# A two-layer decoder trunk on one core: every tile's row in SBUF rounded up to 128 bytes

## Chip, core and metric

The kernel runs on one core of one Trainium2 chip. Its time is what the device takes for one execution, in microseconds (us); the median of the runs counts. Five engines work side by side, each through its own list of instructions: TensorE (matmuls, PE in the rows; the load of a matmul's weights is PEld), VectorE (DVE), ScalarE (ACT), GpSimd (POOL) and SyncE (SP, which here only issues DMAs).

## What is computed

The reference is a decoder trunk with two layers on x of 256 x 1024 in float32. In each layer:

```python
h = rms_norm(x, norm_mix_pre[l])
proj = h @ w_in[l]                       # 1024 x 11776
q, k, v, lru_x, lru_gate, glu_in, gate_logits = jnp.split(proj, IN_SPLITS, axis=-1)
y_a = dilated_attention_mixer(q, k, v, cos, sin, w_o_attn[l])
y_b = rg_lru_mixer(lru_x, lru_gate, ..., w_o_lru[l])
y_c = conformer_conv_mixer(glu_in, conv_dw_w[l], ..., w_o_conv[l])
g = jax.nn.sigmoid(gate_logits).reshape(B, S, N_BRANCHES, D)
merged = g[:, :, 0] * y_a + g[:, :, 1] * y_b + g[:, :, 2] * y_c
x = x + rms_norm(merged @ w_out[l], norm_mix_post[l])
h = rms_norm(x, norm_mlp_pre[l])
u = jnp.square(jax.nn.relu(h @ w_mlp_up[l]))
x = x + rms_norm(u @ w_mlp_down[l], norm_mlp_post[l])
```

Nearly all the arithmetic is in products with weights; about 100 MB of them are read for each layer.

## The kernel before

**Chunks.** The weights come as one stream of 92 chunks a layer, each 128 partitions x 2,048 floats (1 MB). SP loads a chunk into a `raw` buffer (two of them, L428). ScalarE rounds it to the type fp32r, which gives `whi` (L392), and VectorE makes `wlo = raw - whi` (L405); of each there are three buffers. The activations are split in the same way (`hh` and `hl` for h, `uh` and `ul` for the squared ReLU, and so on). Each product is then three fast fp32r matmuls, whi x hi, whi x lo and wlo x hi, summed in PSUM (L452).

**Two shapes of matmul.** In chunks of the kind "ws" (lx, lg, glu, q, k, ga, gb, gc, oa, ob, oc, up: 64 of a layer) the weights are the stationary operand and 256 columns of the activations move past them: 48 matmuls a chunk. In those of the kind "as" (v, wo, ua, dn: 28 of a layer) the activations are stationary and 512 columns of weights move: 24 matmuls a chunk. Every matmul loads 128 columns of its stationary operand. The gate products of the recurrent branch (psr, psi) and the last-but-two chunk of the MLP of layer 0 (dn61, which is kept for later) have their split weights not in `whi` and `wlo` but in general slots. Attention (sc, tp, pv) and the sums of the layer norm are plain fp32 matmuls on smaller tiles; transposes (L459) move `ident` past the data.

**Buffers.** A `Buf` is one logical tile with a tag; all tiles with one tag share that tag's buffers, whose number is `cap[tag]`. The tile is taken from its pool when it is first used, in `View.ap`. The pools lay their buffers one behind another along the row of a partition. `cp` holds constants (x_sb, nhalf with 8 bytes, halfpi with 4, const with 4,100 and others), `wp` raw, whi and wlo, `sp` the rest: gains, xp (2,080 bytes), upad, 24 slots with tag s2 of 2,048 bytes, statistics (tag st, 4 bytes), hh and hl, cpd, sm and pT. `pp` is PSUM.

**Order.** A planner in `Sched.run` simulates the engines with a cost for each operation and writes out one fixed order for each engine, from shapes, costs and the number of buffers; the main matmuls follow a list (`ORDER`). Background work of VectorE and ScalarE, the taps of the convolution with 31 taps, fills the gaps.

Of the kernel before, what the change touches and what calls it, by code (L numbers as in the profile page):

```python
# [100 lines left out]
DMA_RATE = 0.36  # L101
MARGIN = 15000
DMA_ISSUE, DMA_START, DMA_DONE = {"SP": 600, "POOL": 1040, "ACT": 600}, 500, 900
RINGS = ("mm", "tp", "sc", "raw", "whi", "wlo", "upad", "xp", "sm", "pT")


class Buf:
    def __init__(self, sch, pool, shape, dt, tag, name):
        self.sch, self.pool, self.shape, self.dt, self.tag, self.name = sch, pool, shape, dt, tag, name
        self.t = None  # L110
        self.log = []
        self.left = 0
        self.held = False
        self.uses = []

    def __getitem__(self, idx):
        if not isinstance(idx, tuple):
            idx = (idx,)
        reg, n = [], 1
        for i, d in enumerate(self.shape):  # L120
            e = idx[i] if i < len(idx) else slice(None)
            if isinstance(e, int):
                reg.append((e, e + 1))
            else:
                r = range(*e.indices(d))
                reg.append((r[0], r[-1] + 1))
                if i:
                    n *= len(r)
        return View(self, tuple(reg), n, lambda t: t[idx])
# [21 lines left out]
class View:  # L151
# [10 lines left out]
    def ap(self):  # L162
        b = self.buf
        if b.t is None:
            b.t = b.pool.tile(list(b.shape), b.dt, tag=b.tag, name=b.name, bufs=b.sch.cap[b.tag])
        return self.fn(b.t)

    @property
    def psum(self):
        return self.buf.tag in ("mm", "tp", "sc")  # L170


class Op:
# [8 lines left out]
class Sched:  # L182
# [45 lines left out]
    def run(self):  # L228
# [4 lines left out]

        for tag in RINGS:
            ring, c = self.rings[tag], self.cap[tag]
# [1074 lines left out]
```

## Time and profile before

| | us |
|---|---|
| runs | 1141.12 median of 3 (1139.95 to 1143.14) |
| profiled execution, span from its first to its last instruction | 1141.4 |
| TensorE busy in it | 1118.9 |
| VectorE busy | 904.4 |
| ScalarE busy | 720.9 |

The profile shows one execution. What lies around its span is within the spread of the runs: the span and their median differ by 0.3 us. Matmuls overlap, so that a matmul's own duration (about 280 ns for 256 columns) says little; how far the starts of two of them lie apart is what sums to the time.

### The profile page before, as it was taken

Reading aid. Unit: us, or ns where it says so; the run is one execution under the profiler, and the core shown is the slowest. Engines: PE = TensorE matmul, PEld = TensorE weight load, DVE = VectorE, ACT = ScalarE, POOL = GpSimd, SP = SyncE. Lnnn points to the kernel's source line nnn. Section 1 sums busy time; section 2 is a strip of 40 time slices with the busy share of each in tenths; the row PEclk is TensorE's granted clock in tenths of the full one; section 3 lists DMA queues with packets and bytes.
Section 4 is the critical chain, followed back from the end, with each engine's and each line's share of the span. In section 5 each row is a group of like instructions: output and inputs, shape, how many; then the busy total and the mean of one; then the engine's idle time right before and its main releaser. Section 6 shows DMA issues by size and latency. Waiting matters only on the chain.

```text
span 1141.4 us, 20586 instructions
## 1 busy us (share of the span) xinstructions
PE 1118.9 (98%) x8258; PEld 1038.8 (91%) x8258; DVE 904.4 (79%) x1374; ACT 720.9 (63%) x1173; POOL 76.3 (7%) x168
## 2 busy tenths in 40 slices
PE   7999999999999999999999999999999999999995
PEld 6999999999999899989889999999998988889984
DVE  6999999999869865555579999999995888555552
ACT  5779938687765464444468896569776646444441
POOL 1000022111000010000010000221200001000000
PEclk9999999999999999999999999999999999999998
DMA  8654376554345565554455443755624365545541
GB/s 291 237 203 149 146 244 208 185 180 146 129 180 190 186 220 185 184 185 185 184 200 207 168 184 128 252 201 194 214 90 174 136 240 185 187 183 188 193 173 37
DMA packets 37649, 209.76 MB, mean 184 GB/s; under 512 B 6449, under 2 KB 9777, under 8 KB 14130
## 3 DMA queue, kind: packets, MB, share of 16 engines
q1 hardware_dynamic: 32976, 200.05, 49.0%
q0 software_dynamic: 4576, 8.40, 2.2%
q8 instruction: 65, 1.06, 0.4%
q14 instruction: 30, 0.25, 0.1%
q10 hardware_dynamic: 2, 0.00, 0.0%
HBM read 201.08 MB, written 1.05 MB: 177 GB/s over the span
## 4 chain that ended last, share of the span: by engine, by line
PE 83%; DVE 8%; DMA 4%; ACT 3%; issue 1%; SPq 1%; POOL 0%; DVEq 0%; POOLq 0%; ACTq 0%
PE dn L452 16%; PE up L452 14%; PE glu L452 8%; PE v L452 6%; PE gc L452 4%; PE ga L452 4%; PE oc L452 4%; PE lx L452 4%; PE wo L452 4%; PE lg L452 4%; PE k L452 3%; PE oa L452 2%; PE ua L452 2%; PE ob L452 2%; PE pv L452 1%; PE tp L459 1%
## 5 line engine op out<-in xcount | busy, mean ns | idle before, releaser
L405 DVE TENSOR_TENSOR wlo_dn<-raw_dn,whi_dn 128x1024 fp32r<-128x1024 f32 (+1 forms) x66 | 75.8, 1189 | 70.2 <-ACT whi_dn L392 70.2
L392 ACT CAST whi_dn<-raw_dn 128x1024 fp32r<-128x1024 f32 (+1 forms) x66 | 64.4, 1022 | 77.2 <-PE dn L452 45.1
L409 DVE SCALAR_TENSOR_TENSOR c<-upad,parh,c 128x256 f32<-128x256 f32 x256 | 110.3, 477 | 0.1
L452 PE MATMUL up<-hh_mlp,whi_up 128*128 128x256 f32 x448 | 107.7, 280 | 0.0
L452 PE MATMUL up<-hl_mlp,whi_up 128*128 128x256 f32 x448 | 107.6, 279 | 0.0
L452 PE MATMUL dn<-whi_dn,uh 128*128 128x512 f32 x256 | 101.0, 395 | 0.0
L452 PE MATMUL dn<-wlo_dn,uh 128*128 128x512 f32 x256 | 100.8, 394 | 0.0
L405 DVE TENSOR_TENSOR wlo_up<-raw_up,whi_up 128x1024 fp32r<-128x1024 f32 x56 | 66.4, 1221 | 41.6 <-ACT whi_up L392 41.6
L399 ACT ACTIVATE cpd<-upad,parh 128x256 f32<-128x256 f32 x224 | 94.5, 500 | 3.3 <-DVE c L405 3.3
L452 PEld LDWEIGHTS up<-hh_mlp,whi_up 128*128 128x128 f32 x448 | 84.1, 188 | 0.7
L452 PEld LDWEIGHTS up<-hl_mlp,whi_up 128*128 128x128 f32 x448 | 84.0, 188 | 0.6
L392 ACT CAST whi_up<-raw_up 128x1024 fp32r<-128x1024 f32 x56 | 56.2, 1049 | 39.0 <-PE dn L452 21.0
L452 PE MATMUL dn<-whi_dn,ul 128*128 128x512 f32 x256 | 71.6, 394 | 0.0
L405 DVE TENSOR_TENSOR cpd<-cpd 128x1024 f32<-128x1024 f32 (+2 forms) x84 | 63.3, 773 | 0.9 <-ACT cpd L399 0.9
L452 PE MATMUL glu<-hl_mix,whi_glu 128*128 128x256 f32 x256 | 61.7, 279 | 0.0
L452 PE MATMUL glu<-hh_mix,whi_glu 128*128 128x256 f32 x256 | 61.7, 279 | 0.0
L452 PE MATMUL up<-hh_mlp,wlo_up 128*128 128x256 f32 x448 | 61.6, 279 | 0.0
L452 PEld LDWEIGHTS dn<-whi_dn,ul 128*128 128x128 f32 x256 | 47.9, 187 | 11.8
L452 PEld LDWEIGHTS dn<-whi_dn,uh 128*128 128x128 f32 x256 | 47.9, 187 | 11.1
L452 PEld LDWEIGHTS dn<-wlo_dn,uh 128*128 128x128 f32 x256 | 47.9, 187 | 11.0
L452 PEld LDWEIGHTS up<-hh_mlp,wlo_up 128*128 128x128 f32 x448 | 56.5, 188 | 0.0
L452 PEld LDWEIGHTS glu<-hh_mix,whi_glu 128*128 128x128 f32 x256 | 48.0, 188 | 0.0
(306 smaller groups left out, 3399.4 us busy)
## 6 DMA issues: line engine op xcount, KB each, us to landing
raw_dn<-w_in_stream SPq DMA_DIRECT2D x32, 1024.0 KB, 4.8
raw_up<-w_in_stream SPq DMA_DIRECT2D x28, 1024.0 KB, 4.8
raw_glu<-w_in_stream SPq DMA_DIRECT2D x16, 1024.0 KB, 4.8
raw_q<-w_in_stream SPq DMA_DIRECT2D x12, 1024.0 KB, 4.9
raw_k<-w_in_stream SPq DMA_DIRECT2D x12, 1024.0 KB, 4.8
raw_v<-w_in_stream SPq DMA_DIRECT2D x11, 1024.0 KB, 4.8
raw_lx<-w_in_stream SPq DMA_DIRECT2D x8, 1024.0 KB, 4.8
raw_lg<-w_in_stream SPq DMA_DIRECT2D x8, 1024.0 KB, 4.8
```

The costliest lines, as they stand in the source:

```text
L392: nc.scalar.copy(out.ap(), in_.ap())
L399: nc.scalar.activation(out.ap(), in_.ap(), func, scale=val(scale), **kw)
L405: lambda: nc.vector.tensor_tensor(out=out.ap(), in0=a.ap(), in1=b.ap(), op=op), [a, b], [out])
L409: lambda: nc.vector.scalar_tensor_tensor(out=out.ap(), in0=a.ap(), scalar=val(s), in1=b.ap(), op0=op0, op1=op1), [a, b] + views(s), [out])
L452: nc.tensor.matmul(out.ap(), lhsT=lhs.ap(), rhs=rhs.ap(), start=start, stop=stop)
L459: nc.tensor.transpose(out.ap(), a.ap(), ident.all().ap())
```

## The change

Each tile's row in SBUF is made longer until it is a multiple of 128 bytes; the kernel uses the part of the old length through a slice. Tiles in PSUM and the statistics (tag st: 32 buffers) are left as they are. No instruction, shape of an operand or order changes. All tiles of matmuls then begin at a multiple of 128 bytes.

```diff
+LINE = 128
+PSUM_TAGS = ("mm", "tp", "sc")
+UNPADDED = PSUM_TAGS + ("st",)
@@ class Buf
+    def home(self):
+
+        shape, row = list(self.shape), 4
+        for d in shape[1:-1]:
+            row *= d
+        last = shape[-1]
+        while self.tag not in UNPADDED and row * shape[-1] % LINE:
+            shape[-1] += 1
+        t = self.pool.tile(shape, self.dt, tag=self.tag, name=self.name, bufs=self.sch.cap[self.tag])
+        return t if shape[-1] == last else t[(slice(None),) * (len(shape) - 1) + (slice(0, last),)]
@@ class View
     def ap(self):
         b = self.buf
         if b.t is None:
-            b.t = b.pool.tile(list(b.shape), b.dt, tag=b.tag, name=b.name, bufs=b.sch.cap[b.tag])
+            b.t = b.home()
         return self.fn(b.t)
 
     @property
     def psum(self):
-        return self.buf.tag in ("mm", "tp", "sc")
+        return self.buf.tag in PSUM_TAGS
```

## Rows read from the trace of the kernel before

**Rows 1.** The page and the granted clock: span, clock, busy times, chain by engine.
```profile
core 0: 1141.4 us, clock 0.996
...
PE 1118.9 (98%) x8258; PEld 1038.8 (91%) x8258; DVE 904.4 (79%) x1374; ACT 720.9 (63%) x1173; POOL 76.3 (7%) x168
...
PE 83%; DVE 8%; DMA 4%; ACT 3%; issue 1%; SPq 1%; POOL 0%; DVEq 0%; POOLq 0%; ACTq 0%
```
**Rows 2.** The chain in order of time: start us, us, engine, tile, matmuls.
```profile
30.46 28.27 PE glu L452 x240
...
96.95 10.88 PE lg L452 x96
...
243.74 11.31 PE k L452 x96
...
260.70 11.04 PE v L452 x48
...
448.37 11.30 PE up L452 x96
459.68 11.20 PE dn L452 x48
...
802.52 10.88 PE k L452 x96
...
964.21 8.17 PE up L452 x72
```
**Rows 3.** Windows: stretch, its length, busy us by engine, granted clock, DMA.
```profile
20.00:119.00 99.00, 99.00 (x829) 98.09 (x828) 93.45 (x172) 80.58 (x138) 1.53 (x6) 1.00 0.57 207
...
203.00:282.00 79.00, 79.00 (x581) 73.82 (x581) 75.80 (x136) 60.11 (x112) 12.11 (x26) 0.98 0.51 176
...
345.00:425.00 80.00, 80.00 (x500) 71.13 (x499) 67.05 (x91) 42.95 (x64) 6.44 (x10) 1.00 0.55 199
425.00:570.00 145.00, 145.00 (x909) 129.80 (x908) 79.23 (x84) 67.23 (x85) 1.48 (x4) 1.00 0.52 188
...
768.00:845.00 77.00, 77.00 (x590) 71.55 (x589) 76.23 (x138) 60.57 (x116) 11.55 (x24) 1.00 0.54 183
...
982.00:1128.00 146.00, 146.00 (x912) 130.49 (x911) 75.31 (x79) 63.72 (x78) 0.74 (x2) 1.00 0.47 167
```
**Rows 4.** Waits: who waited for whom, us in total, times, longest.
```profile
ACT whi_dn L392 <- PE dn L452: 45.1, 13, 3.6
...
PE sc L452 <- DMA qk<-r1k: 1.8, 1, 1.8
```
**Rows 5.** VectorE's groups with 1,024 and 512 elements, shapes apart.
```profile
L405 DVE TENSOR_TENSOR wlo_dn<-raw_dn,whi_dn 128x1024 fp32r<-128x1024 f32 x62 | 73.4, 1222 | 70.2 <-ACT whi_dn L392 70.2
...
L405 DVE TENSOR_TENSOR ur<-ur 128x512 f32<-128x512 f32 x32 | 21.9, 686 | 1.5 <-ACT ur L399 1.5
```
**Rows 6.** DMA issues: tile, KB each, median us to landing.
```profile
raw_dn<-w_in_stream SPq DMA_DIRECT2D x32, 1024.0 KB, 4.8
```
**Rows 7.** Timeline of TensorE, gate products: first and last of 12 starts.
```profile
95.35 0.28 PE L452 MATMUL psr<-luh,lwh 128*128 128x256 f32 x1
...
96.67 0.28 PE L452 MATMUL psi<-luh,lwl 128*128 128x256 f32 x1
```
**Rows 8.** Timeline of TensorE, dn61: first start and that six later.
```profile
556.52 0.39 PE L452 MATMUL dn<-whi_dn,uh 128*128 128x512 f32 x1
...
557.88 0.39 PE L452 MATMUL dn<-whi_dn,uh 128*128 128x512 f32 x1
```
**Rows 9.** Timeline and group of the attention's transposes.
```profile
222.36 0.60 PE L459 MATMUL tp<-ident,sm 128*128 128x128 f32 x4
...
L459 PE MATMUL tp<-ident,sm 128*128 128x128 f32 x128 | 18.8, 274 | 1.3 <-ACT sm L399 1.3
```
**Rows 10.** The chain in order of time: pieces on VectorE and DMA.
```profile
196.58 6.03 DMA qk<-r1k
...
694.79 4.68 DVE thi L858 x8
```

## Prediction

> **What bounds the kernel now.** I read the clock and span first, then the page's busy shares and chain: TensorE is busy 98% of 1141.4 us at a granted clock of 0.996, and 83% of the chain is its matmuls [rows 1]. At 1.00 the clock is the 2.4 GHz level, so only start-up is lost to it. Second, the chain in order of time [rows 2], for the pace of the matmuls: a piece divided by its count is the spacing of two starts. This is the view that matters, since "busy" hides the pace. A chunk of 1 MB of weights is 48 matmuls of 256 columns or 24 of 512 (one layer: 64 and 28 chunks). At 2.4 GHz, 256 columns are 106.7 ns and 512 are 213.3 ns. Measured: 117.8 ns (glu 28.27/240, up 11.30/96, k 11.31/96), 113.3 ns (lg 10.88/96; k again, 10.88/96, in layer 1), 233.3 ns (dn 11.20/48), 230.0 ns (v 11.04/48) [rows 2]. So TensorE runs 4 to 10% above its column time while it waits for nobody, and k shows two paces for the same instructions on the same buffers. Over the timeline 90 of the 128 chunks with 256 columns keep the slow pace and 38 the fast one, of which the first and the last stand in [rows 2]. Third, the windows [rows 3]: VectorE is 94 to 99% busy from 20 to 119, from 203 to 282 and from 768 to 845 us, and 52 to 55% in the MLP stretches, so only the latter has plenty of room. Fourth, the waits [rows 4]: in the MLP stretch ScalarE waits for TensorE to free buffers (45.1 us before whi_dn), so preparation is ahead there.
>
> **What the change does.** It adds, removes and reorders no instruction, and the planner reads unchanged shapes. What moves is where tiles begin. Before, tiles are laid one behind another in steps of 32 bytes, and the odd rows (nhalf 8 bytes, halfpi 4, const 4,100, xp 2,080) push all later ones off: raw, whi and wlo begin 32 bytes past a multiple of 128, hh, hl, the s2 slots, sm and pT 96 past, ident 64 past. After it each begins at a multiple of 128. The padding is never read, and one row of SBUF grows by about 1.3 KB, which fits.
>
> **Cost on VectorE, ScalarE and DMA: none.** VectorE's step from 512 to 1,024 elements is 1222 - 686 = 536 ns, 1.047 ns an element [rows 5], its 0.96 GHz pace (1.042) within 0.5%; with all operands off the 128-byte grid there is nothing left per element to win. A fixed part may hide one access; bounded by that 0.5% it is 4.5 us of busy time over its 904 us, and I take 0. A chunk lands in 4.8 us [rows 6], below any chunk time here, and two raw buffers overlap; nothing to win either.
>
> **Cost on TensorE.** No row has both operands of a fast matmul on the grid, so I bound it.
> Does the address matter at all? Two places say so. The gate products psr and psi take both operands from s2 slots (both 96 past): 12 starts from 95.35 to 96.79 us (the last listed start, 96.67, plus one more), 120.0 ns each, a pace no other matmul holds for long [rows 7]. And one chunk of layer 0, dn61, keeps its split weights in s2 slots: six starts from 556.52 to 557.88 us, 226.7 ns each, where the same product from whi and wlo takes 233.3 [rows 2, 8]. Same shapes, same engine, other addresses, another pace.
> The excess also has a unit: 113.3 is 17/16 of 106.7, 120.0 is 18/16, 226.7 is 17/16 of 213.3, and 16 columns of fp32 are 64 bytes. Operands that begin 32 bytes off a 64-byte grid, as nearly all do, touch one such block more than they fill. That is my reading: the extra time is extra blocks, of the moving operand or in conflict with the weight load, and it goes when both begin on the grid.
> Price on the grid: at best the column time, 106.7 and 213.3 ns; at worst, if the address helps, the best paces seen, 113.3 and 226.7. The nearest row is the transposes: the moving operand (ident) begins on a 64-byte multiple, 128 weights are loaded each time, and four take 0.60 us with 274 ns for the last, (600 - 274)/3 = 109 ns apart [rows 9]. They are of another kind, but show load and matmul at 2.3 ns above 106.7. I take 106.7 + 2.3 = 109.0 and 213.3 + 2.3 = 215.6 ns.
> The Trainium skill (TensorE: Matmul & The Clock Gate, "Wait — 56ns, not 53.3ns?") gives columns / 2.4 GHz plus about 2.5 ns for back-to-back matmuls. By it the prices would be 109.2 and 215.8, an estimate; no run of before shows it for a fast fp32 matmul, whose rows lie above.
> Sum over both layers, per chunk: 256 columns 48 x 109.0 = 5.23 us against 5.65 (slow) or 5.44 (fast); 512 columns 24 x 215.6 = 5.17 against 5.60 (dn, wo, ua) or 5.52 (v, 8 of its 12 chunks; v0's four are like dn). So 90 x 0.42 = 37.8, 38 x 0.21 = 8.0, 48 x 0.43 = 20.6, 8 x 0.35 = 2.8, and 96 gate products x 11 ns = 1.1: together 70 us.
>
> **What takes part of it back.** A faster TensorE meets the other engines. From 119 to 203 us and from 685 to 768 us the chain runs through VectorE and the q/k copies (thi 4.68 us, a copy of 6.03 us) before a score product can start [rows 10], and TensorE already waits at its end (1.8 us [rows 4]). What it wins there it waits: about 10 fast and 4 slow chunks, 3.8 us, in layer 0, and 8 and 6, 4.2 us, in layer 1. From 203 to 282 and 768 to 845 us VectorE has 3.2 and 0.8 us of idle time [rows 3] and TensorE could win 5.0 (8 slow, 1 fast, 4 of v) and 3.5 (2, 6 and 4): 1.8 and 2.7 lost. From 20 to 119 us VectorE has 93.45 us of work and TensorE would need 99 - 7 = 92: 2 us lost. Together 14.5, say 15 us. What is late next there is VectorE's split of weights (wlo), and behind it the raw buffers and SP's loads. In the MLP (79.23 of 145 us) and the output projections (67.05 of 80) it covers. Net 70 - 15 = 55: 1141.4 - 55 = 1086. The span and the median of the runs (1141.1) differ by 0.3 us, so the time is 1086 too.
>
> **Rivals.**
> *Only the pace flips.* The extra 1/16 is in the fast fp32 matmul itself and the change only ends the conflicts: everything at 113.3 and 226.7. For it: both best paces are exactly 17/16 of the column time. Against: the transposes' 2.3 ns. 90 x 0.21 + 48 x 0.16 + 8 x 0.08 + 0.6 = 28, less 4 taken back: 1117.
> *VectorE absorbs the mixing stage.* Its queue is a fixed order, and every delay there reaches TensorE: only what follows 345 us and 902 us counts, 42 chunks a layer x 0.42 = 35: 1106. For it: 94 to 99% busy. Against: part of that work (the taps) is filler.
> *Nothing happens.* k changes its pace at unchanged addresses [rows 2], so the paces may come from the phase between load and matmul alone: 1141. The Trainium skill (SBUF — State Buffer, "Specifications (TRN2)") speaks for it: it gives lines of 16 bytes, with a penalty for each cross to a new one. Every tile already begins at a multiple of 32, so by that rule nothing changes; the 120.0 against 113.3 and the 226.7 against 233.3 don't agree with it.
> *Slower: equal remainders collide.* psr and psi are the matmuls of 256 columns whose operands have the same remainder, and they are the slowest steady ones, 120.0 [rows 7]. Afterwards all have the same one, 0. Then 90 x 48 x 2.2 ns = 9.6 and 38 x 48 x 6.7 ns = 12.2 are lost, and 48 x 0.16 = 7.7 won at 226.7: +14, 1155. It decides as soon as the 256-column spacing passes about 118. Against: dn61 has equal remainders too, and is faster for it.
>
> **How the numbers follow.** Full gain 0.47 (its own range 1070 to 1101: the lower end is 106.7 and 213.3 for all, 87 us less some 16; the upper is twice the loss), VectorE absorbs 0.09, only the flip 0.17, nothing 0.16, collision 0.11. A measurement of this kernel tells about 0.3%, 3.4 us. Faster 0.47 + 0.09 + 0.17 = 0.73; same 0.16; slower 0.11. The range reaches from 1070 to 1143 and leaves out the collision and some of the edges.
>
> **What would show it.** In the chain, dn should fall from 11.20 to about 10.4 us for 48, up from 11.31 to 10.5 for 96, glu from 28.27 to 26.2 for 240, psr to 109 ns, with no two paces left. VectorE's 1222 ns stays. TensorE's waits should grow before the score products. Wrong: the spacings unchanged (nothing), 113.3 everywhere (flip), 120 (collision), or 109 with a span above 1101 (absorbed).

## The result and the profile after

The changed kernel takes 1151.51 us (median of 4 runs, 1151.07 to 1152.12) against 1140.53 (4 runs, 1139.76 to 1143.14): a ratio of 1.0092, interval 1.0077 to 1.0106. It is slower by 0.9% or 11.0 us and lies above the predicted range, 1070 to 1143. The last rival, that operands with equal remainders collide (1155), comes within 3.5 us.

The page and the granted clock of the changed kernel, the lines that answer to [rows 1]:
```profile
core 0: 1149.6 us, clock 0.996
...
PE 1130.3 (98%) x8258; PEld 1057.6 (92%) x8258; DVE 905.1 (79%) x1374; ACT 721.8 (63%) x1173; POOL 76.2 (7%) x168
...
PE 93%; DVE 2%; ACT 2%; DMA 1%; issue 0%; POOL 0%; SPq 0%; DVEq 0%; POOLq 0%; ACTq 0%
```
The instructions are the same, and so is the mean granted clock. TensorE is busy 11.4 us longer, VectorE and ScalarE less than 1 us longer, and TensorE's share of the chain rises from 83 to 93%: it now sets the pace in stretches where others did.

The chain in order of time, for the pieces of [rows 2] (start, us, engine, tile, matmuls; the line of a matmul is now L466):
```profile
30.49 28.80 PE glu L466 x240
...
98.17 11.52 PE lg L466 x96
...
245.33 11.50 PE k L466 x96
...
451.20 11.51 PE up L466 x96
462.71 10.91 PE dn L466 x48
...
798.75 11.18 PE v L466 x48
809.93 11.50 PE k L466 x96
```
Divide each by its count: glu, lg, k and up all stand at 119.8 to 120.0 ns, where [rows 2] have 117.8 and 113.3. dn falls from 233.3 to 227.3, and k no longer has two paces. v is an exception in part: its chunks v1 and v2 take every second column of the activations as the stationary operand (a stride of 2), and they rise from 230.0 to 232.9 (11.04/48 and 11.18/48). v0 takes adjacent columns and falls with the others; in the timelines the middle spacing of its matmuls in layer 1 goes from 233 to 235 down to 227, where nothing holds it up. The gate products keep their 120.0 ns (in the timeline after, 12 starts from 96.56 to 97.88 us, 1.32 us for 11 steps).

So the two odd pairs of before, [rows 7] and [rows 8], gave the paces of the whole changed kernel but for v1 and v2, to within 0.6 ns.

What the predicted sum called free is free: VectorE's split takes 1223 ns (1222 in [rows 5]), and a chunk still lands in 4.8 us, the row of [rows 6] unchanged. The group after:
```profile
L419 DVE TENSOR_TENSOR wlo_dn<-raw_dn,whi_dn 128x1024 fp32r<-128x1024 f32 x62 | 73.4, 1223 | 69.4 <-ACT whi_dn L406 69.4
```

**Where the time went.** I added up, from the timelines of TensorE of both kernels, each matmul's start to the next start, by tile. A spacing that is over about 0.1 us too long counts as a gap; where exactly that bound lies moves up to 3 us between the rows of one kernel, and some 0.6 us between the differences.

| us, both layers | before | after | difference |
|---|---|---|---|
| 256 columns: glu, lg, lx, q, k, ga, gb, gc, oa, ob, oc, up | 723.2 | 743.9 | +20.6 |
| 512 columns from whi and wlo: dn, wo, ua | 246.4 | 240.4 | -6.0 |
| 512 columns: v | 67.5 | 67.7 | +0.2 |
| score products sc, with the waits inside them | 20.3 | 17.7 | -2.6 |
| gaps behind other main matmuls | 9.3 | 5.1 | -4.2 |

With 0.2 us of small ones this is +8.2, the difference of the two spans (1149.6 and 1141.4). The row of v holds a gain of v0 and a loss of v1 and v2. The medians differ by 11.0. In every run that lists both, the time is 1.7 to 1.9 us above the span; so the profiled execution of before must be its slowest run (1143.14), while 1151.40 after is an ordinary one, and the 0.3 us between span and median before were a coincidence. By the table the matmuls alone would have cost 14.8 us; 6.8 were hidden in time that TensorE had lost before. Two stretches show most of it. Windows (stretch, its length, busy us and instructions of PE, PEld, DVE, ACT and POOL, granted clock, DMA), before:
```profile
119.00:203.00 84.00, 81.49 (x710) 80.20 (x708) 79.82 (x117) 56.69 (x93) 11.98 (x25) 1.00 0.58 199
685.00:768.00 83.00, 81.58 (x709) 80.33 (x708) 79.49 (x125) 50.96 (x78) 12.07 (x25) 1.00 0.57 197
```
and after:
```profile
119.00:203.00 84.00, 84.00 (x705) 83.42 (x704) 79.87 (x119) 58.34 (x95) 11.95 (x25) 1.00 0.56 192
685.00:768.00 83.00, 83.00 (x696) 82.42 (x695) 77.23 (x116) 50.99 (x77) 11.79 (x24) 1.00 0.57 197
```
TensorE's 2.5 and 1.4 us of idle time there are gone, 3.9 of the 6.8. Its list of waits after no longer names sc (1.8 us in [rows 4]) at all; the likely reason is that a slower TensorE arrives when the operands of the score products are ready.

The clock had a part as well. Before, TensorE waited 1.8 us for the operands of a score product, until 202.7 us, and from 202.9 to 206.3 us it was granted half the clock, the 1.2 GHz level; eleven of its matmuls there stand 187 to 214 ns apart, 1.0 us in all above 117.8. After, the same two microseconds run at the 2.4 GHz level (windows as above, before and after):
```profile
204.00:206.00 2.00, 2.00 (x11) 2.00 (x11) 1.94 (x5) 0.76 (x1) 0.00 (x0) 0.50 0.37 147
...
204.00:206.00 2.00, 2.00 (x21) 1.71 (x19) 1.49 (x3) 1.37 (x2) 0.00 (x0) 1.00 0.56 136
```
That 1.0 us is counted under 256 columns before, so at one clock the change costs these chunks some 21.6 us and not 20.6.

### The profile page after: what moved, and what is told of

It reads as the page before. It is cut to its first block, busy times and chain, and to the rows that moved or that the text cites. A ratio compares the mean times of both kernels' runs of the same rounds, so it can differ in the third digit from the quotient of the medians.

```text
span 1149.6 us, 20586 instructions
## 1 busy us (share of the span) xinstructions
PE 1130.3 (98%) x8258; PEld 1057.6 (92%) x8258; DVE 905.1 (79%) x1374; ACT 721.8 (63%) x1173; POOL 76.2 (7%) x168
## 4 chain that ended last, share of the span: by engine, by line
PE 93%; DVE 2%; ACT 2%; DMA 1%; issue 0%; POOL 0%; SPq 0%; DVEq 0%; POOLq 0%; ACTq 0%
PE dn L466 15%; PE up L466 14%; PE glu L466 8%; PE q L466 6%; PE k L466 6%; PE v L466 4%; PE gc L466 4%; PE gb L466 4%; PE ob L466 4%; PE oc L466 4%; PE lg L466 4%; PE lx L466 4%; PE wo L466 4%; PE ga L466 3%; PE oa L466 2%; PE ua L466 2%
## 5 line engine op out<-in xcount | busy, mean ns | idle before, releaser
L466 PE MATMUL up<-hh_mlp,whi_up 128*128 128x256 f32 x448 | 110.0, 283 | 0.0
L466 PE MATMUL up<-hl_mlp,whi_up 128*128 128x256 f32 x448 | 109.9, 283 | 0.0
L466 PE MATMUL dn<-whi_dn,uh 128*128 128x512 f32 x256 | 99.8, 390 | 0.0
L466 PE MATMUL dn<-wlo_dn,uh 128*128 128x512 f32 x256 | 99.8, 390 | 0.0
L466 PEld LDWEIGHTS up<-hl_mlp,whi_up 128*128 128x128 f32 x448 | 85.9, 192 | 0.5
L466 PEld LDWEIGHTS up<-hh_mlp,whi_up 128*128 128x128 f32 x448 | 85.9, 192 | 0.6
L466 PE MATMUL dn<-whi_dn,ul 128*128 128x512 f32 x256 | 70.1, 389 | 0.0
L466 PE MATMUL up<-hh_mlp,wlo_up 128*128 128x256 f32 x448 | 62.9, 283 | 0.0
L466 PE MATMUL glu<-hh_mix,whi_glu 128*128 128x256 f32 x256 | 62.8, 283 | 0.0
L466 PE MATMUL glu<-hl_mix,whi_glu 128*128 128x256 f32 x256 | 62.8, 283 | 0.0
L466 PEld LDWEIGHTS up<-hh_mlp,wlo_up 128*128 128x128 f32 x448 | 57.8, 192 | 0.0
L466 PEld LDWEIGHTS dn<-whi_dn,ul 128*128 128x128 f32 x256 | 48.1, 188 | 10.0
L466 PEld LDWEIGHTS dn<-wlo_dn,uh 128*128 128x128 f32 x256 | 48.1, 188 | 9.6
L466 PEld LDWEIGHTS dn<-whi_dn,uh 128*128 128x128 f32 x256 | 48.1, 188 | 9.5
L466 PEld LDWEIGHTS glu<-hh_mix,whi_glu 128*128 128x128 f32 x256 | 49.2, 192 | 0.0
```

Source lines behind the costliest of these rows:

```text
L466: nc.tensor.matmul(out.ap(), lhsT=lhs.ap(), rhs=rhs.ap(), start=start, stop=stop)
```

## The experiments

Below, the *distance* of a matmul is the byte in the row where its moving operand begins minus that where its stationary operand begins, modulo 256. Before, weights lie 32 and activations 96 past a multiple of 128, which in these layouts makes the distance 64 for the chunks with 256 columns (weights stationary) and 192 for those with 512 (activations stationary). For psr, psi and dn61 it is 0. After the change it is 0 for all, but for half of the matmuls of v1 and v2, whose stationary columns begin 4 bytes later. (The change promises multiples of 128 only, and so a distance of 0 or 128; that it is 0 follows from the sizes of the tiles, which put whi, wlo, hh, hl and the slots all at a multiple of 256.) One theory is then that the pace follows from the distance; its rival is that it follows from the place on a grid.

**1. The disputed cost by itself, over 12 starts.** A kernel of 41 blocks of 48 matmuls with 256 columns or 24 with 512, back to back, in fp32r, executed once; both operands walk through their tiles in steps that are multiples of 512 bytes:
```python
k = r % 7
s0, m0 = so // 4 + k * P, mo // 4 + k * n
nc.tensor.matmul(o, lhsT=W[:, s0:s0 + P], rhs=M[:, m0:m0 + n], start=r == 0, stop=r == reps - 1)
```


> The disputed cost by itself: the kernel computes nothing of the reference but runs 34 blocks of fast fp32r matmuls back to back (48 of 256 columns or 24 of 512), in which the stationary operand begins s bytes and the moving one m bytes past a multiple of 128. Theory 'distance': only m - s counts. Blocks with m = s all alike (120.0 ns for 256 columns, 226.7 ns for 512), whatever s is; blocks with m - s = 64 at 113.3 or 117.8 ns and 233.3 ns. Theory 'place': each operand's own place counts; then m = s = 32 or 96 differs from m = s = 0, and s = 0, m = 64 differs from s = 64, m = 0. For the other distances neither theory has a number; I guess 113 to 120.

The chain in order of time. A block's name is its columns (n 256, w 512), the stationary and the moving operand's start (a 0, b 16, e 64, g 96, h 112, j 192, k 256):
```profile
32.12 5.65 PE n_a_e L44 x48
...
49.29 5.44 PE n_a_h L44 x48
...
60.42 5.45 PE n_a_j L44 x48
65.87 5.74 PE n_a_k L44 x48
...
77.31 5.44 PE w_a_a L44 x24
...
127.30 5.60 PE w_a_j L44 x24
...
143.96 5.67 PE n_b_b L44 x48
...
166.78 5.75 PE n_g_g L44 x48
172.53 5.59 PE w_b_b L44 x24
...
216.79 5.75 PE n_a_a L44 x48
```
With 256 columns, 48 take 5.74 to 5.75 us (119.7 ns a piece) when both begin at 0, at 96 (and at 32 and 64), or at 0 and 256. At distance 64 they take 117.7, at 112 and 192 113.3 to 113.5. With 512 columns distance 0 is the best of all twelve starts: 226.7, against 229.6 at 64 (5.51/24) and 233.3 at 192. No block is below 113.3 or 226.7. So the pace does not need the kernel around it, and distance 0 is the best case for 512 columns and, with 80 and 96 (5.76 us each), the worst for 256.

The expectation that equal starts are alike wherever they lie holds only for multiples of 32. With both operands at 16 or at 48, 256 columns take 118.1 and 117.9 (5.67 and 5.66 us) and 512 take 232.9 and 230.0 (5.59 and 5.52), although the distance is 0. All tiles of both kernels begin at multiples of 32; within 32 bytes the place counts too.

**2 and 3. Place or distance, in the kernel.** Two versions of the changed kernel that only lengthen one tile further:
```diff
+EXTRA = {"cosT": 8}        # all_32_past;  {"gb": 8} in activations_64_past
...
         while self.tag not in UNPADDED and row * shape[-1] % LINE:
             shape[-1] += 1
+        shape[-1] += EXTRA.get(self.tag, 0)
```
The first shifts weights and activations alike by 32 bytes: off the grid, distance 0. The second shifts the activations alone to a multiple of 64, not of 128: distances 64 and 192, as before the change.

> The changed kernel with one constant's row 32 bytes longer, so that raw, whi, wlo, hh, hl, the slots, sm and pT all begin 32 bytes past a multiple of 128: equal places, off the 128-byte grid. Theory 'distance': the same as the changed kernel, 120.0 ns for 256 columns and 226.7 ns for 512, about 1151 us. Theory 'place' (a beginning on the grid is what slows the 256-column matmuls): the spacing leaves 120.0, back to 113 to 118 ns, 1142 us or less.

> The changed kernel with the two gain buffers 32 bytes longer each, so that all of the activations (hh, hl, slots) begin 64 bytes past a multiple of 128 while whi and wlo stay on it: the distance of the kernel before, with operands on 64-byte multiples. Theory 'distance': the paces of before, 113.3 or 117.8 ns and 233.3 ns, 1141 us within 3. Theory 'place' (operands off 64-byte multiples cost an extra block, on them they don't): 109 ns and 216 ns, or with the stationary or the moving operand at 0 still 120 ns: 1150 us.

| | us, median (runs) | against before | ratio, interval |
|---|---|---|---|
| all_32_past | 1152.27 (1151.61 to 1155.01) | 1141.56 | 1.0098, 1.0077 to 1.0118 |
| activations_64_past | 1143.91 (1141.16 to 1148.8) | 1141.56 | 1.0021, 1.0005 to 1.0037 |

The chain of all_32_past:
```profile
31.34 28.80 PE glu L468 x240
...
419.10 10.91 PE dn L468 x48
```
and of activations_64_past:
```profile
30.73 28.27 PE glu L468 x240
...
413.83 11.20 PE dn L468 x48
425.04 11.30 PE up L468 x96
```
Off the 128-byte grid with equal remainders the kernel is as slow as the changed one, pace for pace. With the old distances the old paces come back (28.27, 11.20, 11.30), although every operand now begins at a multiple of 64. That it stays 2.4 us above before goes with its fast chunks: about 20 of 128 instead of 38. Both expectations of the distance theory are met, and the theory of the grid falls.

**4. Finer distances, and what the unit could be.** The same kernel as in 1 with other offsets, and with blocks that use 64 columns of weights instead of 128 or move 384 columns.

> Again only blocks of fast fp32r matmuls, at other distances between the beginnings of the moving and the stationary operand, and with other shapes; nothing of the reference is computed. Theory 'distance modulo 256': 192 gives 113.3 ns for 256 columns from every base (0, 32, 96), 448 the same as 192, 320 the same as 64; 512 columns at 64 give about 229 ns from bases 32 and 96. Rival 'history': the pace of a block follows the block before it; then the three blocks at 64 after different blocks differ, and 192 isn't always 113.3. Loading 64 stationary columns in place of 128 leaves half of the reads of weights out: if the two reads collide, 256 columns come down to 107 to 110 ns and 512 to 214 to 217; if 1/16 belongs to the moving operand alone, they stay at 113.3 and 226.7.

The chain (here d 32, f 96, k 192, m 224, o 288; h is 256 columns past 64 columns of weights):
```profile
38.56 5.45 PE n_a_k L46 x48
...
133.75 5.45 PE n_d_m L46 x48
139.19 5.65 PE n_f_o L46 x48
144.85 5.60 PE w_d_f L46 x24
...
178.48 5.65 PE n_a_k L46 x48
...
189.79 5.60 PE h_a_a L46 x48
195.39 5.44 PE h_a_e L46 x48
200.83 5.71 PE h_a_k L46 x48
```
Distance 192 gives 113.5 ns here at 38.56 us, and 117.7 at 178.48 us between two blocks with distance 64: one distance, two paces, and the same pair as in [rows 2] for k. Starts at 32 and 224 (distance 192) take 113.5 as well, but starts at 96 and 288, the same distance, take 117.7 in the very next block. 512 columns at distance 64 do likewise: 233.3 from 32 and 96, 228.8 from 96 and 160 (5.49/24). So the expectation that a distance gives one pace from every base failed twice, and what was called the rival, history, is needed as well. For 512 columns, 240 is about as good as 0 (227.1 with the start of the block, 226.7 later).

Half the weights change the pace of 256 columns (116.7 at distance 0, 113.3 at 64, 119.0 at 192) but don't lower the best. 512 columns become slower at distance 0 by it (230.0, 5.52/24, against 226.7), and 384 columns with all weights take 173.3 to 175 ns at all three distances, where the column time would be 160. Neither of the two forecasts for half the weights came true. Each such block ran once behind one other block, so history may have a part in these numbers; they show that the time above the column time is not the weights' volume alone, and no more.

**5 to 7. The change in halves, and the opposite choice for each shape.** whi and wlo get rows 256 bytes longer, and a chunk uses them from another start according to its kind; activations stay at a multiple of 256:
```diff
+WS_PAST, AS_PAST, ROOM = 0, 192, 256   # narrow_part_alone; 192, 0 wide_part_alone; 64, 0 best_distances
...
+        split = self.tag in ("whi", "wlo")
+        if split:
+            shape[-1] += ROOM // 4
...
+        if split:
+            kind = self.name.split("_")[1]
+            o = (AS_PAST if kind[0] == "v" or kind[:2] in ("wo", "ua", "dn") else WS_PAST) // 4
+            return t[:, o:o + last]
```
The distances (256 columns, 512 columns) are 0 and 192, 64 and 0, 192 and 0.

> The changed kernel with whi and wlo in rows 256 bytes longer; chunks whose weights are stationary use them from 0 past (distance 0, as after the change), chunks whose weights move from 192 past (distance 192, as before the change). Theory 'distance': 120.0 ns for 256 columns, 233.3 for 512: the loss of the change without its gain, 1141 + 22 = 1163 us. Rival 'something else in the padding cost the time': about 1151.

> The same with stationary weights from 192 past (distance of the activations 64, as before the change) and moving weights from 0 past (distance 0, as after it). Theory 'distance': 117.8 or 113.3 ns for 256 columns, 226.7 for 512: the gain of the change without its loss, 1141 - 8 = 1133 us. Rival 'something else in the padding cost the time': about 1151.

> The same with stationary weights from 64 past (the activations then begin 192 further modulo 256) and moving weights from 0 past. Theory 'distance modulo 256': 113.3 ns everywhere for 256 columns and 226.7 for 512; 90 slow chunks x 0.21 and 48 x 0.16 us, 27 us, less some 4 that the other engines take back: 1118 us. Rival 'history' (113.3 comes only after certain other matmuls): 117.8 for many, 1133 us.

| | us, median (runs) | against before | ratio, interval |
|---|---|---|---|
| narrow_part_alone | 1158.68 (1157.97 to 1160.0) | 1141.65 | 1.015, 1.013 to 1.0169 |
| wide_part_alone | 1136.04 (1135.57 to 1138.23) | 1141.65 | 0.9952, 0.9933 to 0.9971 |
| best_distances | 1134.48 (1133.54 to 1135.56) | 1141.65 | 0.9937, 0.9918 to 0.9956 |

The chain of narrow_part_alone:
```profile
420.09 11.21 PE dn L474 x48
431.29 11.51 PE up L474 x96
```
of wide_part_alone:
```profile
411.04 10.89 PE dn L474 x48
421.93 11.30 PE up L474 x96
```
and of best_distances:
```profile
241.14 10.88 PE k L474 x96
...
410.13 10.90 PE dn L474 x48
421.03 11.31 PE up L474 x96
```
The halves are +17.0 and -5.6 us, together +11.4 where the whole change has +11.0. One change thus holds a loss and a gain with one cause. best_distances should have brought all 256-column chunks to 113.3 if the distance alone set the pace; up stays at 117.8 behind dn at 226.7, lg too, and only some 29 chunks are fast. So the chunks before seem to count as well, and the expectation of 1133 for that case is met.

**8 and 9. A distance that doesn't depend on history?** sweep_history puts blocks of 36 behind forerunners of different kinds (distance 0, distance 64, 512 columns); distance_112 is the code of 5 to 7 with `144, 0`.

> Blocks of fast fp32r matmuls again, nothing of the reference. Seven distances (96, 104, 108, 112, 116, 120, 240) with 256 columns, each after three different forerunners (distance 0, distance 64, 512 columns at distance 0), then 64 and 192 after 112. Theory 'each distance has its pace, but 64 and 192 have two that hold themselves': 112 goes at 113.3 ns after every forerunner, and 64 and 192 right after it stay at 113.3 instead of 117.8. Rival '113.3 is only a matter of the block before': 112 also falls to 117 or more after one of the three.

> The kernel with the best distances, but the stationary weights from 144 past in place of 64, so that the activations begin 112 further modulo 256; moving weights stay at distance 0. If 112 always goes at 113.3 ns: some 96 slow chunks win 0.21 us each against best_distances, 20 us, less up to 5 taken back by the other engines: about 1119 us. If the pace only follows what went before: 117 to 120 ns again, 1134 to 1142 us.

The chain of sweep_history (here a 0, b 64, g 112, j 192): a block at 112, short blocks at 64 behind 112 and behind 120, and the two long ones at 64 and 192 behind 112:
```profile
69.83 4.14 PE n_a_g L45 x36
73.97 1.88 PE n_a_b L45 x16
...
112.94 1.82 PE n_a_b L45 x16
...
147.27 5.65 PE n_a_b L45 x48
...
156.71 5.46 PE n_a_j L45 x48
```
The forerunners at distance 64 show the two paces and the history by themselves: 1.82 us for 16 (113.8 ns, 113.3 after the first) behind blocks at 96 and at 120, and 1.88 to 1.89 (117.8 after the first) behind 104, 108, 112, 116 and 240. Behind 112, 64 keeps 117.7 and 192 gets 113.8; half of that expectation failed. In blocks, 112 settles at 113.3 behind all three forerunners after 9 to 11 matmuls (a mean of 115 with the start, 4.14/36). In the kernel it doesn't: 1149.23 us (1148.97 to 1149.61) against 1140.73, ratio 1.0073, interval 1.0054 to 1.0092. The chain of distance_112 has about 120 (11.52/96) in most chunks and 118.3 in others:
```profile
111.78 11.36 PE lg L474 x96
...
428.45 11.51 PE up L474 x96
```
This expectation failed: 1149 lies above both of its cases. The sweeps' operands lie at multiples of 512 plus the offset, while the kernel's rows of 8,448 bytes (8,192 and the 256 of room) make the distance 112 and 368 modulo 512 in turn. Whether that is the reason isn't shown; the next pair asks about modulo 512, but at the distances 192 and 64.

**10 and 11. Modulus 256 or 512, and both shapes off their worst.** The weights stay where the change put them, and the activations begin 192 or 448 bytes further than they do, modulo 512. Modulo 256 the distance is 192 for 256 columns and 64 for 512 columns in both. The edit is that of 2 and 3 with another number:
```diff
+EXTRA = {"gb": 56}         # activations_192_of_512;  {"gb": 24} in activations_448_of_512
```


> The changed kernel with the gain buffers longer, so that all activations begin 192 bytes further than whi and wlo modulo 512: distance 192 for 256 columns, 320 (64 modulo 256) for 512 columns. 512 columns: 228.9 ns (as at 64 and 320 in the blocks), 5 us won against the kernel before. 256 columns: if the modulus is 256 and the block before decides between the two paces, a mix of 117.8 and 113.3 as before, some 1137 us; if the fast pace belongs to 192 modulo 512 (it was 113.3 in four of the five blocks at 192, and 117.8 in the one at 448), 113.3 everywhere and about 1120 us.

> The same with 448 in place of 192 (64 for 512 columns). Modulus 256: the same as activations_192_of_512 within 4 us. Modulus 512: 117.8 ns everywhere, 1141 + 38 x 0.21 - 5 = 1144 us.

Measured: 1131.21 (1128.61 to 1135.89) and 1131.33 (1129.37 to 1133.87) against 1141.95; ratios 0.991 (0.9883 to 0.9937) and 0.9901 (0.9884 to 0.9917). The chain of activations_192_of_512:
```profile
30.75 27.20 PE glu L468 x240
...
409.64 10.99 PE dn L468 x48
420.62 10.91 PE up L468 x96
```
and of activations_448_of_512:
```profile
30.55 28.27 PE glu L468 x240
...
423.85 10.91 PE up L468 x96
```
The two medians are equal, and neither forecast of modulus 512 came true (up is at 113.6 in both, and in the timelines lg is at 117.8 in both), so 256 is modulus enough for the time. Both beat both kernels, by 0.9 to 1.0% against before. In both, dn at 228.9 (11.0/48) goes with up at 113.6, where dn at 226.7 in best_distances goes with up at 117.8: giving 2 ns of dn for 4 of up is the better trade. glu runs at 113.3 in the one profiled execution and at 117.8 in the other, 1.07 us apart in this piece. The one is the fastest of its four runs and the other the slowest of its own; whether the cause is 192 against 448 or chance isn't shown.

## Why the prediction was wrong

**What bounds the kernel**: right. TensorE's spacing of starts, not its busy share, was the view that showed the loss (98% in both). Two readings were off without effect: the excess over the column time is 6 to 10%, not 4 to 10, and the clock lost more than the start-up, as the 0.98 in the second window of [rows 3] says (202.9 to 206.3 us at half the clock).

**That the address matters**: right, and [rows 7] and [rows 8] were its whole evidence. Each of them forecast the changed kernel to 0.6 ns: 120.0 and 226.7.

**VectorE, ScalarE, DMA at no cost**: right, by 1223 against 1222 ns and 4.8 us.

**The price on the grid**: this step failed, in the words "it goes when both begin on the grid". The sum took 109.0 and 215.6 ns, which no run shows; measured were 120.0 and 227.3, and the best paces anywhere are 113.3 and 226.7. The counted unit of 64 bytes was read as a property of one operand against a grid; the runs show one of the pair, since 32/32 and 96/96 are as 0/0, and the old distances on 64-byte multiples bring the old paces. Thus for the 128 chunks of 256 columns the term had the wrong sign (some 46 us of gain forecast, 20.6 of loss measured), and for 512 columns it was too large (20.6 us of gain forecast, 6.0 measured). The nearest row I took for the price, the transposes [rows 9], is another kind of matmul, and the prediction said so; rows of the right kind, with equal remainders, were at hand and said 120.0.

The Trainium skill (TensorE: Matmul & The Clock Gate, "Wait — 56ns, not 53.3ns?") would have the matmuls at columns / 2.4 GHz plus about 2.5 ns, an estimate of 109.2 ns for 256 columns and 215.8 for 512. No run here agrees with that for fp32r, whose best are 113.3 and 226.7.

**What takes part back**: the sign was turned with the rest, but the place was right. The waits before the score products, 119 to 203 and 685 to 768 us, are what a change of TensorE's pace is settled against: 3.9 of the 14.8 us lost went into them in the profiled executions, and 2.9 into others. The step from the span to the time rested on a coincidence: the time is some 1.8 us longer.

**The rivals.** *Equal remainders collide* was the case, with its mechanism (equal remainders of both operands), its place (all 256-column chunks) and its signs. Its terms: 9.6 (the product is 9.5) + 12.2 = 21.8 us of loss, measured 20.6, or 21.6 at one clock; 7.7 of gain at 226.7, measured 6.0 less 0.2 for v. Its waits were taken as zero, and they hid 6.8. What was held against it, that dn61 has equal remainders and is faster, is no objection: sweep and halves show that one distance is bad for 256 columns and good for 512. A chance of 0.11 was too low for the one rival whose paces stood in rows of the kernel itself. *Nothing happens* leaned on k's two paces at unchanged addresses. The two paces at one address are real, but which can occur depends on the distance: 64 and 192 hold either, and at 0 all 128 chunks of the changed kernel hold one. The Trainium skill (SBUF — State Buffer, "Specifications (TRN2)"), with its lines of 16 bytes and a penalty for each cross to a new one, gives no reason for a change when all tiles begin at multiples of 32; 1151.5 against 1140.5 us disagrees. *Only the pace flips* has its 226.7 for dn, and its 113.3 at other distances than 0. *VectorE absorbs* wasn't tested, since TensorE became slower.

**What stays open.** Why distances 64 and 192 hold two paces, and what hands one on, isn't shown; the runs show only that the block before matters. That the two reads of the operands collide would fit a pace that follows from their distance, but no run shows such a collision. Nor is it shown why 16/16 and 48/48 differ from 0/0, where the last sixteenth above the column time comes from, or why 112 holds 113.3 in blocks and not in the kernel.

## What to carry to other kernels

For back-to-back fp32r matmuls whose operands begin at multiples of 32 bytes it isn't alignment to 128 that counts but the distance of the moving from the stationary operand: before aligning, list the pairs of operands that already have the remainders which the change would give to all, and take their spacing of starts as the price. Price each shape by itself, since one distance can be the worst for one and the best for another. Try a layout in the kernel itself, because what a block leaves behind sets the pace of the next, and in the medians the best distance for each shape alone (1134.5 us) lost to a compromise (1131.2), though single runs of the two overlap.

## What the runs showed of the hardware

The spacing of back-to-back fp32r matmuls depends on the distance between its two operands in the row. In blocks at the 2.4 GHz level with nothing waited for, it ranges from 113.3 (5.44/48, distance 112) to 122.5 ns (4.41/36, distance 116) for 256 columns, and from 226.7 (5.44/24, distance 0) to 237.1 (5.69/24, distance 4) for 512. Distance 0 settles at 120.0 and 226.7 where both operands begin at a multiple of 32. 64 and 192 hold one of two paces: 113.3 or 117.8 for 256 columns at either; for 512 columns 228.9 or 233.3 at 64 (both in the blocks, and both for wo in activations_192_of_512, 20.63/90 and 21.00/90). Near 112 a few bytes matter: 113.3 at 112, 119 to 120 at 108, 122.5 at 116. With 64 columns of weights instead of 128, in one block each, 256 columns take 116.7 at distance 0 and 119 at 192.
